# A two-layer encoder: rotated copies, last-head loads, token chunks and strips issued at other places

## The chip, the cores and the metric

The kernel runs on one core of one Trainium2 chip. The metric is the device time of one execution in microseconds (us); the median of several runs is compared. The core has a matrix engine (TensorE, PE in the profile), a vector engine (DVE), a scalar or activation engine (ACT), a general engine (POOL) and a queue engine (SP) that issues nearly all the DMAs here. Each engine works through its own instructions strictly in the order in which they were put there. An instruction that waits therefore holds up everything behind it on that engine.

## The reference

Two layers over 1024 tokens of width 1024: differential attention with eight heads, then latent attention with eight heads. Each ends in an output projection, a gate and a residual add; a final RMSNorm closes the trunk.

```python
for i in range(DEPTH):
    shift, scale, gate = _modulation(c, ada_w[i], ada_b[i])
    h = _rmsnorm(x, norm_g[i]) * (1.0 + scale) + shift
    y = _diff_attention(...) if i == 0 else _mla(...)
    x = x + gate * y
return _rmsnorm(x, final_norm_g)

def _diff_attention(h, ...):
    q, k, v, z = jnp.split(h @ w_in, 4, axis=-1)   # q and k: two parts of 64 per head, rotated (rope)
    sc = einsum(q, k) * scale
    p = softmax(sc)
    p = p[:, :, 0] - lam * p[:, :, 1]
    o = rmsnorm(p @ v, subln_g) * (1.0 - lambda_init) * silu(z)
    return o @ w_out
```

## The kernel before, in words

**Arithmetic.** A float32 product is made of three matmuls on parts: each operand is split into a high part (a cast on ACT) and a low part (a subtraction, mostly on POOL), and `mm3` (L182 to L184) adds high by high, low by high and high by low. A triple of 128x512 matmuls is the unit in which PE's work is counted below.

**First layer.** The heads, counted from 0, run one after the other. While PE computes scores (L851), transposes of probabilities (L383) and products with the values (`pv`) of head h, a stream of projection triples (`acc`) for head h+1 is mixed in. Each weight strip is fetched by SP (L206), cast on ACT (`wh`, L227) and subtracted on POOL (`wl`, L228). For one row tile of 128 queries, two halves of the softmax follow each other: scores `s` on PE, the maximum on DVE (`nm`, L400), the exponential on ACT (L402), and then DVE joins the two (`e`, L859).

**Rotation.** When half of a head's k or q projection is done, `rope` starts: ACT copies the accumulator out (`rp_raw`), SP issues four DMAs that exchange rows (`rp_sw`, L323), POOL multiplies (L324, L329) and, from head 1 on, adds (L331). Then `stack_q` or `stack_k` makes the operands of the scores: two ACT copies (`qa`, L352 and L353), two POOL subtractions (`qb`, L354 and L355) and four DMAs on SP (L357 and L358, for qa and qb). The scores of a head wait for these DMAs.

**Order.** The steps of a rotation are entries of one list, `side`; each step of the projection stream (one triple) takes one entry off it. An entry `None` passes one step by. From head 1 on, a half puts ten entries on the list, for eight steps of its stream. `hooks` is a second list that is run at later points of the attention loop. Marked instructions keep the program's order on their engine (`in_turn`, `behind`).

**First output projection.** The first layer's `o @ w_out` is computed with seven half-size products instead of eight (class `Seven`, object `sv0`). Operands are fetched (`fetch_a`, `fetch_w`) and split (`split_a`, `split_w`: ACT cast L1173, POOL subtraction L1174; `oah`/`oal` from the attention output, `woh`/`wol` from the weights). `extra0(i)` issues this during the last head of the first layer, step i of eleven; `PRE0[i]` says how many triples of product 0 PE does in that step. When the products are done, `add0` adds them on DVE to the residual (`x`, L1390), `group0` normalises four token tiles (DVE L457 and ACT L455) and puts eight chunks on `side`. A chunk is four transposes on PE (`trh`, L468), an ACT pass (`h1_h`, L473) and a DVE pass with a subtraction (L477, L478). `G_WAIT` empty entries stand ahead of them. Two banks serve the transposes. During product 6 the list is stepped every second triple. The second layer's strips (`w_s1`) are fetched and split here too.

**Elsewhere.** `store_v` casts a tile of values, subtracts and stores it. `load_wk(h)` loads and splits weights for the second layer's keys and values. `qp_done` is the rotation of the second layer's q. At the end `add_to` adds up the last row tiles and `rsqrt8k` computes the root on DVE in seven small instructions; `rsqrt` does it with one power on POOL.

## Time and profile before

| | |
|---|---|
| median of 3 runs | 1430.78 us (1428.41 to 1431.87) |
| profiled execution | 1428.76 us; its span 1427.0 us |
| PE busy | 1382.6 us, 97% of the span, 7350 matmuls |
| DVE / ACT / POOL busy | 937.9 / 737.0 / 751.1 us |
| mean granted TensorE clock | 0.988 |
| bytes moved | 231.55 MB, mean 162 GB/s |

The profiled execution lasted 1.76 us longer than the span that its trace shows. In a timeline row stand the start, the duration, the engine, the line, the operation with output and inputs, and in brackets how long the engine was idle before and what ended that. In a row of the waits stand the engine and operation that waited, what it waited for, and then the total in us, the number of times and the longest. In a row of windows stand the stretch, its length, the busy time of each engine with its number of instructions, the granted clock as a share of full speed, the DMA share and GB/s.

### The profile page before, as it was taken

The numbers are of one execution on the slowest core, as the hardware profiler recorded it, in microseconds if no ns is written. First come the engines' busy times: TensorE is split into PE (matmuls) and PEld (weight loads), VectorE is DVE, ScalarE is ACT, GpSimd is POOL, SyncE is SP. The second block draws the span as 40 slices with busy tenths as digits, with TensorE's granted clock in tenths as the row PEclk, the third lists the DMA queues.
The fourth block names the chain that finished last, engine by engine and source line by source line (L and its number), as shares of the span: only waits on it lengthen the run. The fifth ranks groups of instructions, "written<-read, shape, count | busy, mean of one in ns | idle before, by whom it ended". The sixth has DMA issues, their size and how long they took to land. (4 is left out here: it accounts for less than half of the span.)

```text
span 1427.0 us, 20754 instructions
## 1 busy us (share of the span) xinstructions
PE 1382.6 (97%) x7350; PEld 1154.4 (81%) x7350; DVE 937.9 (66%) x1345; ACT 737.0 (52%) x1331; POOL 751.1 (53%) x589
## 2 busy tenths in 40 slices
PE   8999999999999999999898999999999999999997
PEld 6777788888888787887786888787888888888886
DVE  8665777777666665667496886545665655555685
ACT  5523455656565555566546443335454454545554
POOL 5415274758686767674694233632131165653783
PEclk8999999999999999999999999999999999999999
DMA  9776634343444343525564136498444355566463
GB/s 339 252 241 193 201 104 129 91 132 104 151 125 138 119 136 108 161 62 185 160 231 157 43 87 217 127 302 240 156 124 120 103 165 185 182 211 204 144 243 119
DMA packets 149067, 231.55 MB, mean 162 GB/s; under 512 B 20577, under 2 KB 57569, under 8 KB 148962
## 3 DMA queue, kind: packets, MB, share of 16 engines
q1 hardware_dynamic: 148962, 230.21, 51.2%
q8 instruction: 58, 0.95, 0.3%
q14 instruction: 47, 0.39, 0.1%
HBM read 144.74 MB, written 61.81 MB: 145 GB/s over the span
## 5 line engine op out<-in xcount | busy, mean ns | idle before, releaser
L385 ACT CAST pth<-tr 128x512 fp32r<-128x512 f32 x256 | 150.2, 587 | 298.2 <-PE tr L383 296.3
L400 DVE TENSOR_REDUCE nm<-s 128x1 f32<-128x1024 f32 x192 | 233.9, 1219 | 98.5 <-PE s L851 86.7
L386 DVE TENSOR_TENSOR ptl<-tr,pth 128x512 fp32r<-128x512 f32 x256 | 176.3, 688 | 146.9 <-ACT pth L385 144.8
L228 POOL TENSOR_TENSOR wl<-wraw,wh 128x512 fp32r<-128x512 f32 (+2 forms) x79 | 103.0, 1305 | 200.6 <-ACT wh L227 176.9
L402 ACT ACTIVATE e<-s,nm 128x1024 f32<-128x1024 f32 x128 | 143.5, 1121 | 35.0 <-DVE nm L400 31.6
L383 PE MATMUL tr<-ident,e 128*128 128x128 f32 x1024 | 156.5, 275 | 3.3 <-DVE ptl L386 3.3
L383 PEld LDWEIGHTS tr<-ident,e 128*128 128x128 f32 x1024 | 122.3, 141 | 45.8 <-DVE ptl L386 21.2
L182 PE MATMUL acc<-h0h,wh 128*128 128x512 f32 x360 | 151.4, 420 | 0.4 <-DVE v_hl L363 0.3
L182 PE MATMUL pv<-pth,vt 128*128 128x256 f32 x512 | 147.4, 288 | 0.0
L183 PE MATMUL pv<-ptl,vt 128*128 128x256 f32 x512 | 145.6, 284 | 0.0
L184 PE MATMUL pv<-pth,vt 128*128 128x256 f32 x512 | 144.6, 282 | 0.0
L184 PE MATMUL acc<-h0h,wl 128*128 128x512 f32 x360 | 143.1, 398 | 0.8 <-POOL wl L228 0.8
L183 PE MATMUL acc<-h0l,wh 128*128 128x512 f32 x360 | 142.1, 395 | 0.0
L324 POOL TENSOR_TENSOR rp_r<-rp_raw,cosT 128x512 f32<-128x512 f32 x38 | 49.7, 1309 | 103.4 <-ACT rp_raw L321 43.8
L183 PEld LDWEIGHTS pv<-ptl,vt 128*128 128x128 f32 x512 | 97.7, 191 | 3.0
L182 PEld LDWEIGHTS pv<-pth,vt 128*128 128x128 f32 x512 | 97.6, 191 | 2.9
L184 PEld LDWEIGHTS pv<-pth,vt 128*128 128x128 f32 x512 | 97.6, 191 | 0.1
L851 PE MATMUL s<-ks,qa 128*128 128x512 f32 x256 | 84.2, 410 | 11.6 <-DMA qa<-qa 6.9
L1174 POOL TENSOR_TENSOR wol<-wol,woh 128x512 fp32r<-128x512 f32 x56 | 82.2, 1490 | 21.2 <-ACT woh L1173 21.1
L859 DVE SCALAR_TENSOR_TENSOR e<-s,z,e 128x1024 f32<-128x1024 f32 x64 | 82.2, 1284 | 2.2
L851 PE MATMUL s<-ks,qb 128*128 128x512 f32 x256 | 81.2, 398 | 0.5 <-DMA qb<-qb 0.5
L184 PEld LDWEIGHTS acc<-h0h,wl 128*128 128x128 f32 x360 | 67.7, 188 | 16.7 <-POOL wl L228 1.3
(410 smaller groups left out, 3477.4 us busy)
## 6 DMA issues: line engine op xcount, KB each, us to landing
ada<-in_ada_ss SPq DMA_DIRECT2D x32, 512.0 KB, 5.6
wraw<-in_w_s SPq DMA_DIRECT2D x64, 256.0 KB, 2.9
vS<-v_hl SPq DMA_DIRECT2D x32, 512.0 KB, 5.9
vt<-vS SPq DMA_DIRECT2D x32, 512.0 KB, 4.9
wol<-tS SPq DMA_DIRECT2D x56, 256.0 KB, 5.1
tS<-ob SPq DMA_DIRECT2D x48, 256.0 KB, 2.0
rp_sw<-rp_raw SPq DMA_DIRECT2D x168, 64.0 KB, 2.0
bc_s<-bc_d SPq DMA_DIRECT2D x34, 256.0 KB, 3.9
```

The costliest lines, as they stand in the source:

```text
L182: PE.matmul(psum, ah, bh, start=first, stop=False, skip_group_check=skip)
L183: PE.matmul(psum, ah, bl, start=False, stop=False, skip_group_check=skip)
L184: mm3.last = PE.matmul(psum, al, bh, start=False, stop=last, skip_group_check=skip).ins
L228: sub = (V if pair_of else G).tensor_sub(l_[:, :n], raw[:, :n], f32v(h_[:, :n]))
L383: transpose_p.last = PE.transpose(tr[:, j, :], p[:, kt * P : (kt + 1) * P], ident).ins
L385: mk["S"] = S.copy(pth[kh][:, :, dst], tr).ins
L386: mk["V"] = V.tensor_sub(ptl[kh][:, :, dst], tr, f32v(pth[kh][:, :, dst])).ins
L400: mk["V"] = V.reduce_max(nm, s_ps, axis=AX.X, negate=True).ins
L402: mk["S"] = S.activation(e, s_ps, AF.Exp, bias=nm, scale=1.0, accum_out=zs).ins
L851: PE.matmul(s_ps[:, kc * HF : (kc + 1) * HF], src[:, c, ql], KS[h][kc][:, c, :], start=fst, stop=not fst)
L859: combined.append(V.scalar_tensor_tensor(out=e0, in0=e1, scalar=z1[:, 0:1], in1=e0, op0=ALU.mult, op1=ALU.add).ins)
L1174: sub = eng.tensor_sub(lo, raw, f32v(hi))
```

## The change

The edits, with their places:

- `k_done`, `q_done`: the two entries `sum_` are gone, so the copies come two steps sooner.
- `extra0`, `PRE0`, `head_out`: the first fetches of product 0 stand one step earlier, splits are issued at other steps, and the last head's first root (`rest`) is issued behind the splits of its step instead of in `hooks`.
- `G_WAIT` from 3 to 5; the first two strips of `w_s1` are fetched together, two tiles in the buffers `wraw`, two in those of `gz`.
- `store_v` of the first v tiles uses six buffers of another tag; halves of q are projected one v tile later; two tags of the pool `a0b` are allocated ahead.
- `load_wk(1)` moves behind a later part of the same stage; the rotation's add of `qp_done` is on POOL for head 0, half 1.
- The last row tile's root is a power on POOL.

```diff
-PRE0 = (0, 0, 0, 0, 1, 2, 2, 2, 2, 2, 3)
+PRE0 = (0, 0, 0, 0, 1, 2, 2, 2, 3, 2, 2)
-G_WAIT = 3
+G_WAIT = 5
-        store_v(0, p1b, vacc[tt], 4 + tt, 0)
+        store_v(0, p1, vacc[tt], 4 + tt, 0, "xt", 6)
...
-                stack_q(qa, qb, r.pop() if r else fin())
+                stack_q(qa, qb, fin())
                 QS.setdefault(h, [None, None])[half] = qa, qb
-            r = []
-            sum_ = [lambda: r.append(fin()), None] if h else []
-            side.add(*[None] * ROT, rot, *[None] * (DEF - 1 - ROT), *sum_, g)
+            side.add(*[None] * ROT, rot, *[None] * (DEF - 1 - ROT), g)
...
-        for t in pend[4 + 2 * tt : 6 + 2 * tt]:
+        for t in pend[2 + 2 * tt : 4 + 2 * tt] if tt else ():
...
-        if dst is None and h < NH - 1:
-            hooks.append(rest)
+        if dst is None:
+            (hooks if h < NH - 1 else rests).append(rest)
...
+        if i == 1:
+            sv0.fetch_w(0, 0)
...
-            for h in range(2):
-                fw(0, h)
-                fa(0, h)
+            fa(0, 0, 1)
+            fw(0, 1)
+            sv.split_w(0, 0)
         if i == 3:
+            sv.split_a(0, 0, G)
...
-        for n, h in ((), (), (), ((0, 0),), ((0, 1), (0, 2)), ((0, 3), (1, 0)), ((1, 1),), ((1, 2),), (), (), ())[i]:
+        for n, h in ((), (), (), (), ((0, 1), (0, 2)), ((0, 3),), ((1, 0), (1, 1)), ((1, 2),), (), (), ())[i]:
             both(n, h)
+        while rests:
+            rests.pop(0)()
...
             if i == 1 and n == 5:
+                raws = [[], []]
                 with tc.issue_after(w6):
-                    raws = fetch_strip([A["w_s1"][0, f] for f in range(2)], [4, 4])
-            if i == 0 and n == 6:
-                w4.append(split_strip(raws))
-            if i == 1 and n == 6:
-                raws = fetch_strip([A["w_s1"][1, f] for f in range(2)], [4, 4])
-            if i == 3 and n == 6:
-                w4.append(split_strip(raws, h1p))
+                    for k, (tag, nb) in enumerate((("wraw", 2), ("gz", 3))):
+                        for f in range(2):
+                            raw = wst.tile([P, HF], F32, name="wraw", tag=tag, bufs=nb)
+                            SP.dma_start(raw, A["w_s1"][k, f])
+                            raws[k].append((raw, 4))
+            if i > 1 and n == 6:
+                w4.append(split_strip(raws.pop(0), h1p if i == 3 else None))
...
+            load_wk(1)
     z_pair(1)
-    load_wk(1)
...
-            rot, fin = rope(wp, acc, half, SC1)
+            rot, fin = rope(wp, acc, half, SC1, G, V if h or not half else G)
...
-        if early:
+        if tt == NT - 1:
+            y = rsqrt(w, 1)
+            G.tensor_scalar(y, y, -8192.0, None, op0=ALU.mult)
+            scale(tt, y[:, 0:1])
+        elif early:
             scale(tt, rsqrt8k(w)[:, 0:1])
```

The lines of the kernel after are shifted by up to eight against the kernel before.

SP ahead of head 4, in the kernel before: `qa_4113` and `qb_4114` are the first half's operands, `rp_sw_4101` the second half's exchanged rows.

```order
L206 DMA wraw_4074<-in_w_s0 128x512
L323 DMA rp_sw_4101<-rp_raw_4100 32x512 x4
L357 DMA qa_4113<-qa_4113 64x512
L358 DMA qa_4113<-qa_4113 64x512
L357 DMA qb_4114<-qb_4114 64x512
L358 DMA qb_4114<-qb_4114 64x512
```

The same stretch of SP now, with `qa_4078` and `qb_4079` for the first half:

```order
L206 DMA wraw_4076<-in_w_s0 128x512
L357 DMA qa_4078<-qa_4078 64x512
L358 DMA qa_4078<-qa_4078 64x512
L357 DMA qb_4079<-qb_4079 64x512
L358 DMA qb_4079<-qb_4079 64x512
L323 DMA rp_sw_4113<-rp_raw_4112 32x512 x4
```

The first half's four DMAs now stand ahead of the second half's four exchanges.

ACT at the same place before, where `e_4050` and `s_4076` are the two exponentials of one row tile:

```order
L402 ACTIVATE e_4050,zz_3860<-s_4043,nm_4048 128x1024
L227 CAST wh_4068<-wraw_3835 128x512
L385 CAST pth_3980<-tr_4090 128x4x128
L402 ACTIVATE s_4076,z1_4042<-s_4076,nm_4081 128x1024
L321 ACTIVATE rp_raw_4100<-acc_3991 128x512
L352 CAST qa_4113<-rp_r_3968 64x512
L353 CAST qa_4113<-rp_r_3968 64x512
```

And now:

```order
L402 ACTIVATE e_4052,zz_3862<-s_4045,nm_4050 128x1024
L227 CAST wh_4070<-wraw_3837 128x512
L352 CAST qa_4078<-rp_r_3975 64x512
L353 CAST qa_4078<-rp_r_3975 64x512
L385 CAST pth_3982<-tr_4102 128x4x128
L402 ACTIVATE s_4088,z1_4044<-s_4088,nm_4093 128x1024
L321 ACTIVATE rp_raw_4112<-acc_3993 128x512
```

The two copies, which read POOL's sum, moved ahead of the cast of transposed probabilities and of the second exponential.

POOL in the last head before, where `rq_y` is the root and `wol_6758` the low part that a triple of product 0 reads:

```order
L919 TENSOR_TENSOR o_6890<-o_6890,gz_6486 128x512
L169 TENSOR_TENSOR rq_y_6905<-sl_w_6899,mhalf_109 128x4
L934 TENSOR_TENSOR rq_y_6905<-rq_y_6905,sl_f_6900 128x4
L1174 TENSOR_TENSOR oal_6913<-k11_6666,oah_6912 128x512
L1174 TENSOR_TENSOR wol_6758<-wol_6758,woh_6757 128x512
```

And now, with `wol_6764` for the same part:

```order
L917 TENSOR_TENSOR o_6892<-o_6892,gz_6498 128x512
L1172 TENSOR_TENSOR oal_6898<-k11_6671,oah_6897 128x512
L1172 TENSOR_TENSOR wol_6764<-wol_6764,woh_6763 128x512
L169 TENSOR_TENSOR rq_y_6913<-sl_w_6907,mhalf_109 128x4
L932 TENSOR_TENSOR rq_y_6913<-rq_y_6913,sl_f_6908 128x4
```

The two subtractions passed the root.

ACT around the first chunks in the first output projection before, where `wh_7815` to `wh_7923` belong to the first two strips and `wh_8213` to the third:

```order
L227 CAST wh_7815<-wraw_7713 128x512
L227 CAST wh_7819<-wraw_7715 128x512
L473 ACTIVATE h1_h_7729<-trh_7731,modb1_105,moda1_104 128x512
L1394 ACTIVATE tjunk_7742,ss1_7182<-x0_6_7177 128x512
L473 ACTIVATE h1_h_7759<-trh_7761,modb1_105,moda1_104 128x512
L227 CAST wh_7919<-wraw_7861 128x512
L1394 ACTIVATE tjunk_7775,ss1_7182<-x0_7_7178 128x512
L227 CAST wh_7923<-wraw_7863 128x512
L473 ACTIVATE h1_h_7783<-trh_7785,modb1_105,moda1_104 128x512
L227 CAST wh_8213<-wraw_8209 128x512
```

And now, where `wraw_8211` is the third strip's raw tile:

```order
L227 CAST wh_7875<-wraw_7715 128x512
L227 CAST wh_7921<-wraw_7719 128x512
L227 CAST wh_7879<-wraw_7717 128x512
L1397 ACTIVATE tjunk_7737,ss1_7184<-x0_6_7179 128x512
L227 CAST wh_7925<-wraw_7721 128x512
L227 CAST wh_8215<-wraw_8211 128x512
L1397 ACTIVATE tjunk_7759,ss1_7184<-x0_7_7180 128x512
L473 ACTIVATE h1_h_7767<-trh_7769,modb1_105,moda1_104 128x512
```

All of the casts, the third strip's first one too, now stand ahead of the first chunk's pass.

## The prediction

> **What bounds the kernel now.** I read the top of the page first, then the waits of PE, then the granted clock in short windows behind PE's longest pauses, and last the timelines of the engines at each pause.

> ```profile
> span 1427.0 us, 20754 instructions
> PE 1382.6 (97%) x7350; PEld 1154.4 (81%) x7350; DVE 937.9 (66%) x1345; ACT 737.0 (52%) x1331; POOL 751.1 (53%) x589
> ```

> PE is busy for 1382.6 of 1427.0 us, and no edit adds or removes a matmul. The change can act only on the 44.4 us in which PE stands, and on stretches in which it runs slowly. The waits of PE (in all, times, longest) say what ends the pauses:

> ```profile
> PE s L851 <- DMA qa<-qa: 6.9, 4, 2.9
> PE tr L383 <- DVE ptl L386: 3.3, 6, 0.9
> PE s L851 <- DVE e L859: 3.2, 3, 2.4
> PE oy L183 <- POOL wol L1174: 2.5, 1, 2.5
> PE vps L182 <- DVE v_hl L363: 1.7, 1, 1.7
> PE vps L182 <- DVE gz L786: 1.4, 1, 1.4
> PE zacc L184 <- POOL wl L228: 0.9, 1, 0.9
> PE s L851 <- DMA qb<-qb: 0.5, 1, 0.5
> ```

> The first and last rows are the starts of heads 4 to 7, 7.4 us together. The third and fourth are mostly the last head. Some pauses cost more than themselves, as the windows after two of them show (the third figure from the right is the granted clock), and the length of the matmuls themselves:

> ```profile
> 490.00:492.50 2.50, 2.44 (x13) 2.03 (x14) 0.43 (x1) 0.11 (x1) 2.32 (x2) 1.00 0.06 18
> 562.00:564.00 2.00, 2.00 (x7) 1.43 (x6) 0.00 (x0) 0.00 (x0) 1.92 (x2) 0.50 0.37 139
> 564.00:566.00 2.00, 2.00 (x11) 1.67 (x11) 0.95 (x1) 0.59 (x1) 0.55 (x1) 0.86 0.00 0
> ```

> ```profile
> 490.06 0.70 PE L851 MATMUL s<-ks,qa 128*128 128x512 f32 x2 [2.24 <-DMA qa<-qa]
> 561.51 1.19 PE L851 MATMUL s<-ks,qa 128*128 128x512 f32 x2 [2.93 <-DMA qa<-qa]
> 663.55 1.22 PE L851 MATMUL s<-ks,qa 128*128 128x512 f32 x2 [2.40 <-DVE e L859]
> 683.55 0.50 PE L183 MATMUL oy<-wol,oah 128*128 128x512 f32 x1 [2.52 <-POOL wol L1174]
> 684.62 1.05 PE L851 MATMUL s<-ks,qa 128*128 128x512 f32 x2
> ```

> A pause of 2.24 us left the clock at 1.00, and a pair of score matmuls took 0.70 us. After 2.93 us the clock was 0.50, and the pair took 1.19; it took 1.22 after 2.40 us, and 1.05 just behind the pause of 2.52. So those three pauses were followed by half clock. From the two windows after 562 such a stretch loses 2 x 0.50 + 2 x 0.14 = 1.3 us, and I use 1.3 us for each of the three. [...]

> **The change, part by part: the rotation's copies.** In the four waits of 6.9 us and the one of 0.5 us, the four DMAs stood on SP behind the second half's exchanges, and POOL's subtractions behind its next multiplication:

> ```profile
> 556.30 1.29 POOL L355 TENSOR_TENSOR qb<-rp_r,qa 64x512 fp32r<-64x512 f32 x1
> 557.85 0.59 SPq L358 DMA_DIRECT2D qa<-qa  x1
> ```

> Now both subtractions pass that multiplication, which is of their own size (1.29), so they end at 556.3 instead of 557.6, and qa is issued as soon as ACT has copied. PE stood ready at 558.58 (561.51 less 2.93). The last of qa was issued at 557.85 and let PE start at 561.51, 3.7 us later; by that, a qb issued at 556.3 arrives near 560.0, and PE asks for it 0.5 us after qa, at 559.1. I leave 0.3 of the wait (0 to 0.9, since at 419 one wait for qb was as short as 0.5). The gain is 7.4 - 0.3 = 7.1 us, and the cold stretch after 561 goes, 1.3 more: 8.4.

> The copies also pass instructions on ACT, and there they can wait for POOL's sum L331. Head 4 is the place:

> ```profile
> 404.08 0.62 ACT L227 CAST wh<-wraw 128x512 fp32r<-128x512 f32 x1
> 406.44 1.10 ACT L402 ACTIVATE s<-s,nm 128x1024 f32<-128x1024 f32 x1
> 407.47 1.28 POOL L331 TENSOR_TENSOR rp_r<-rp_r,rp_sw 128x512 f32<-128x512 f32 x1
> 411.02 0.63 PE L851 MATMUL s<-ks,qa 128*128 128x512 f32 x2
> ```

> POOL's order ahead of L331 is unchanged in length, so ACT, free at 404.70, stands until 408.75. Two copies of 0.62, a cast of 0.58 and the exponential (1.1, read-out 0.2) follow: it ends near 411.8 instead of 407.7. Queued behind it are DVE's join L859 (some 1.7 with its small steps) and the scores of 411.02, which need its bank: 413.5. That is a new pause of 2.5 us (0 if POOL comes sooner, 4.2 and a cold stretch of 1.3 at worst). At head 6 the same move costs nothing:

> ```profile
> 549.94 1.30 POOL L331 TENSOR_TENSOR rp_r<-rp_r,rp_sw 128x512 f32<-128x512 f32 x1
> 553.45 1.12 ACT L402 ACTIVATE e<-s,nm 128x1024 f32<-128x1024 f32 x1
> ```

> The sum is there at 551.24, two copies end at 552.5, ahead of the exponential at 553.45. Part one: 8.4 - 2.5 = **+5.9** saved (2.3 to 8.7).

> **The last head.** Two stalls, each with a cold stretch behind it:

> ```profile
> 659.94 0.62 ACT L1173 CAST woh<-wol 128x512 fp32r<-128x512 f32 x1 [0.80 <-DMA wol<-tS]
> 660.47 1.08 ACT L402 ACTIVATE s<-s,nm 128x1024 f32<-128x1024 f32 x1
> 679.77 1.01 POOL L169 TENSOR_TENSOR rq_y<-sl_w,mhalf 128x4 f32<-128x4 f32 x1 [2.04 <-DVE sl_w L932]
> 682.82 1.28 DVE L859 SCALAR_TENSOR_TENSOR e<-s,z,e 128x1024 f32<-128x1024 f32 x1
> ```

> The cast waited 0.80 us for its DMA in front of an exponential that could have begun at 659.14. With the fetch a step earlier it stands ahead of the exponential before, so DVE's join and the scores of 663.55 come 1.33 us sooner. The 1.07 us pause that stays is below 2.24, so I drop its cold stretch: 1.3 + 1.3. At 683.55 PE waited for `wol`, behind a root that waited for DVE. The subtractions now pass the root; but the scores behind that triple need the bank that DVE frees at 682.82 + 1.28 = 684.10, against 684.62. Of 2.52 us only 0.5 becomes time, and a pause near 2.0 stays, at which I drop the second cold stretch too. Part two: 1.3 + 1.3 + 0.5 + 1.3 = **+4.4** (1.8 if the clock still falls at both, 7 if the chain also moves up).

> **The first output projection.**

> ```profile
> 759.76 3.43 DVE L457 TENSOR_SCALAR x<-x,rq_y 128x1024 f32<-128x1024 f32 x2 [1.20 <-POOL rq_y L169]
> 763.12 1.87 DVE L1390 TENSOR_TENSOR x<-x,oy 128x512 f32<-128x512 f32 x3
> 763.59 0.78 PE L182 MATMUL oy<-woh,oah 128*128 128x512 f32 x1
> 771.31 0.47 PE L182 MATMUL oy<-woh,oah 128*128 128x512 f32 x1
> 771.78 0.62 ACT L227 CAST wh<-wraw 128x512 fp32r<-128x512 f32 x1 [2.33 <-DMA wraw<-in_w_s]
> 776.54 0.66 PE L468 MATMUL trh<-ident,x 128*128 128x128 f32 x4 [1.77 <-DVE h L477]
> 786.01 0.40 PE L182 MATMUL acc<-h_h,wh 128*128 128x512 f32 x1
> ```

> Today two pauses of PE on L457 stand ahead of 763.59. They go as waits, but product 6 cannot begin before DVE's first add has freed its bank, a third of the way through the row at 763.12: near 763.7, as now. One pause of some 4 us takes the place of two.

> Two triples then precede each group of transposes. Now PE got from 763.59 to 771.31 with five triples and two groups, most of it at a slow clock; six and two bring it to the third group at 772.0. That group needs a bank that ACT's first pass and then DVE's must free, and ACT's pass now stands behind the third strip's cast. Now that cast waited until 771.78 for a buffer and its DMA, and POOL still frees the buffer behind the same subtractions. With a pass on each engine behind it, some 0.8 each, the bank is free near 774.8: a pause of 2.8 us, cold after it, 1.3. From the row at 776.54 to the strip at 786.01 PE needed 9.5 us for four groups and ten triples; six groups and ten triples (a group is 0.35 more) reach the strip at 785.0. So 1.0 saved and 1.3 lost: **-0.3** (-3.5 if the cold stretch is as long as the one after 763.59, +2 if the DMA lands sooner).

> **The rest.** `load_wk(1)` and the add on POOL take the work away that stood ahead of the waits of 0.9 and 1.7 us: 2.6 at most, **+2.0** since DVE gets two casts elsewhere (0 to 2.6). The stores of the first v tiles and the later halves of q bear on the 1.4 us wait on gz: **+0.5** (-1 to +2). For the last root:

> ```profile
> L169 POOL TENSOR_TENSOR rq_y<-xss,mhalf 128x1 f32<-128x1 f32 x1 | 0.6, 553 | 0.0
> 1419.38 0.16 DVE L2173 SCALAR_TENSOR_TENSOR tw<-tss,tw 128x1 f32<-128x1 f32 x1
> 1421.90 0.75 DVE L2187 SCALAR_TENSOR_TENSOR x<-x,rq_y,fg 128x512 f32<-128x512 f32 x1
> ```

> POOL, idle there, takes 0.55 and a short multiply from 1419.54, ready near 1420.4. Both rows' products (0.75 each) then end about 0.5 sooner than 1422.65: **+0.5** (-0.5 to 0.8). Against all this I set new small waits, since every head's order changed; the present ones on ptl are 3.3 us in six: **-1.5** (-4 to 0).

> **The sum.** 5.9 + 4.4 - 0.3 + 2.0 + 0.5 + 0.5 - 1.5 = 11.5 us saved. Against the profiled execution's 1428.76 us (its span and 1.76 us around it) that is 1417.3; it lay 2.0 below the median of the three runs, so **1419.3 us** as a median. The parts' bounds, taken as independent of each other, make about 1414.6 to 1426.2 of this case.

> **Rivals.** *The softmax chain takes over (0.12).* At heads 5 to 7 the scores, no longer late for qa, wait for DVE's join instead, as at 684. For it: the 3.2 us on L859. Against: while streams run, those waits are only in the last head. Part one's 8.4 is lost: 11.5 - 8.4 = 3.1, 1427.7, no measurable change.

> *The third strip's cast blocks more (0.13).* If its DMA lands later than 771.78, both banks stay taken: 2 us more pause and a cold stretch twice as long make about -5 instead of -0.3, so 6.8 saved, 1424.0.

> *ACT stands at many heads (0.11, slower).* The pause of head 4, 2.5 with a cold stretch of 1.3, recurs at the moved copies of k and q, fourteen places. It decides where ACT arrives more than the 1.6 us of slack (411.02 less 409.4, the join's end) ahead of POOL's sum. Five further places and head 4's own cold stretch cost 5 x 3.8 + 1.3 = 20.3, leaving 8.8 us more than before: 1439.6; with three it is no change. For it: POOL's sum comes 4 us late at head 4. Against: head 6 above.

> *The copies are not really sooner (0.06).* POOL or SP still sets qb's landing and only half of the 8.4 is had: 7.3 saved, 1423.5.

> **How the numbers follow.** The forecast has 0.58. A measurement here tells a change from none at about 0.3%, 4.3 us. Faster: 0.58 + 0.13 + 0.06 = 0.77; the same: 0.12; slower: 0.11. The range runs from 1410, below the case's own 1414.6 by what a warm first projection and no head-4 pause would add together, to 1430, which takes in every case but the slower one.

> **What would show it.** Right: no wait on DMA qa above 1 us, clock 1.00 in the windows after heads 6 and 7 begin and after 663 and 684, no wait of PE on `wol`. A pause of about 2.5 us near 411 on L859, while head 3 runs, with ACT idle before L352 on POOL L331. One pause of 4 us at 760 and one near 772 on the transposes. Wrong: waits on L859 at the starts of heads 5 to 7, ACT idle on L331 at several heads, or half clock where I dropped it.

## The result, and the profile after

The kernel after took 1431.31 us (median of 14 runs, 1428.85 to 1436.29), the kernel before 1431.09 us (14 runs on the same chips). The ratio is 1.0001, with a 95% interval of 0.9988 to 1.0015: no change that can be measured. The forecast was 1419.3 us, with a range of 1410 to 1430.

The top of the page and PE's waits of the kernel after (in all, times, longest):

```profile
span 1426.9 us, 20750 instructions
PE 1380.7 (97%) x7350; PEld 1150.1 (81%) x7350; DVE 937.0 (66%) x1337; ACT 737.9 (52%) x1331; POOL 753.9 (53%) x592
```

```profile
PE tr L383 <- DVE ptl L386: 9.7, 11, 2.2
PE trh L468 <- DVE h L477: 4.5, 1, 4.5
PE s L847 <- DVE e L855: 4.1, 7, 1.0
PE ssq L924 <- ACT rp_raw L321: 2.5, 1, 2.5
...
PE vps L182 <- DVE gz L782: 1.3, 1, 1.3
```

The waits on DMA qa (6.9 us) are gone, as forecast, and of the wait on `wol` (2.5 us) 0.6 us is left, at two places. In their place PE waits on `ptl`, the low part of the transposed probabilities: 9.7 us instead of 3.3. The cause stands in the waits of ACT, of before first and then of after:

```profile
ACT qa L352 <- POOL rp_r L331: 2.2, 2, 1.6
ACT ks L344 <- POOL rp_r L331: 1.0, 2, 0.7
```

```profile
ACT qa L352 <- POOL rp_r L331: 23.3, 11, 4.8
ACT ks L344 <- POOL rp_r L331: 8.2, 5, 3.4
```

ACT now stands 31.5 us at 16 places ahead of a moved copy, because POOL's sum is not there yet. One place, in head 0 while head 1's q is rotated, shows how that reaches PE. The timeline of the kernel before, and then of the kernel after:

```profile
206.60 1.12 ACT L402 ACTIVATE e<-s,nm 128x1024 f32<-128x1024 f32 x1 [0.61 <-DVE nm L400]
206.71 1.28 POOL L331 TENSOR_TENSOR rp_r<-rp_r,rp_sw 128x512 f32<-128x512 f32 x1
...
210.74 0.62 ACT L352 CAST qa<-rp_r 64x512 fp32r<-64x512 f32 x1
```

```profile
206.51 0.59 ACT L385 CAST pth<-tr 128x512 fp32r<-128x512 f32 x1 [2.67 <-PE tr L383]
...
210.57 1.29 POOL L331 TENSOR_TENSOR rp_r<-rp_r,rp_sw 128x512 f32<-128x512 f32 x1
...
211.90 0.62 ACT L352 CAST qa<-rp_r 64x512 fp32r<-64x512 f32 x1 [4.80 <-POOL rp_r L331]
...
212.42 1.11 ACT L402 ACTIVATE e<-s,nm 128x1024 f32<-128x1024 f32 x1
...
214.28 1.09 ACT L402 ACTIVATE s<-s,nm 128x1024 f32<-128x1024 f32 x1
...
216.13 1.28 DVE L855 SCALAR_TENSOR_TENSOR e<-s,z,e 128x1024 f32<-128x1024 f32 x1
...
217.33 0.68 DVE L386 TENSOR_TENSOR ptl<-tr,pth 128x512 fp32r<-128x512 f32 x1
...
218.07 0.66 PE L383 MATMUL tr<-ident,e 128*128 128x128 f32 x4 [2.24 <-DVE ptl L386]
```

Before, both exponentials stood ahead of the copy, and by then the sum was long there. After, ACT waits 4.80 us for it with both exponentials queued behind: their maxima (`nm`, L400 on DVE) ended at 208.64 and 210.37, and they started only at 212.42 and 214.28. DVE's join, `ptl` and PE's transposes follow late, and PE stands 2.24 us.

The sum itself also came later: it began at 206.71 before and at 210.57 after. It needs the exchanged rows, and their DMAs now stand on SP behind the first half's `qb`, which waits for the first half's subtractions. SP's issues, before first and then after:

```profile
199.79 2.42 SPq L323 DMA_DIRECT2D rp_sw<-rp_raw  x4
```

```profile
204.64 0.46 SPq L358 DMA_DIRECT2D qb<-qb  x1
205.20 2.44 SPq L323 DMA_DIRECT2D rp_sw<-rp_raw  x4
```

The exchanges went out 5.4 us later, of which 1.1 us is the later start of the heads. So at this place the move did two things: it put the copy ahead of the exponentials, and it made the sum late that the copy waits for.

What the eight heads cost is read from a landmark: the distance from the first product with the values of head 0 to that of head 7. Before it is 654.69 - 174.33 = 480.36 us, after it is 487.23. The rows of the kernel after:

```profile
175.43 0.28 PE L182 MATMUL pv<-pth,vt 128*128 128x256 f32 x1
...
662.66 0.36 PE L182 MATMUL pv<-pth,vt 128*128 128x256 f32 x1
```

So the heads lost 6.9 us where I forecast a gain of 5.9, and the other parts of the change gave it back.

### The profile page after: what moved, and what is told of

It reads as the page before. It is cut to its first block, busy times and chain, and to the rows that moved or that the text cites. A ratio compares the mean times of both kernels' runs of the same rounds, so it can differ in the third digit from the quotient of the medians.

```text
span 1426.9 us, 20750 instructions
## 1 busy us (share of the span) xinstructions
PE 1380.7 (97%) x7350; PEld 1150.1 (81%) x7350; DVE 937.0 (66%) x1337; ACT 737.9 (52%) x1331; POOL 753.9 (53%) x592
## 4 chain that ended last, share of the span: by engine, by line
PE 70%; DVE 5%; POOL 5%; ACT 3%; DMA 3%; issue 2%; SPq 2%; POOLq 0%; ACTq 0%; DVEq 0%
PE s L1986 10%; PE acc L182 8%; PE acc L184 8%; PE acc L183 8%; PE tr L383 7%; PE s L847 6%; PE pv L182 3%; PE pv L184 3%; PE pv L183 3%; PE zacc L184 1%; PE zacc L183 1%; PE zacc L182 1%; PE oy L184 1%; PE oy L182 1%; PE oy L183 1%
## 5 line engine op out<-in xcount | busy, mean ns | idle before, releaser
L400 DVE TENSOR_REDUCE nm<-s 128x1 f32<-128x1024 f32 x192 | 233.9, 1219 | 77.4 <-PE s L847 68.1
L386 DVE TENSOR_TENSOR ptl<-tr,pth 128x512 fp32r<-128x512 f32 x256 | 176.1, 688 | 148.5 <-ACT pth L385 147.9
L228 POOL TENSOR_TENSOR wl<-wraw,wh 128x512 fp32r<-128x512 f32 (+2 forms) x79 | 102.1, 1295 | 185.0 <-ACT wh L227 180.8
L383 PE MATMUL tr<-ident,e 128*128 128x128 f32 x1024 | 155.8, 274 | 10.0 <-DVE ptl L386 9.7
L383 PEld LDWEIGHTS tr<-ident,e 128*128 128x128 f32 x1024 | 120.4, 140 | 54.3 <-DVE ptl L386 31.5
L402 ACT ACTIVATE e<-s,nm 128x1024 f32<-128x1024 f32 x128 | 143.6, 1121 | 26.5 <-DVE nm L400 26.2
L182 PE MATMUL acc<-h0h,wh 128*128 128x512 f32 x360 | 150.6, 418 | 0.1
L182 PE MATMUL pv<-pth,vt 128*128 128x256 f32 x512 | 147.5, 288 | 0.0
L183 PE MATMUL pv<-ptl,vt 128*128 128x256 f32 x512 | 145.5, 284 | 0.0
L184 PE MATMUL pv<-pth,vt 128*128 128x256 f32 x512 | 144.6, 282 | 0.0
L184 PE MATMUL acc<-h0h,wl 128*128 128x512 f32 x360 | 143.2, 398 | 0.4 <-POOL wl L228 0.4
L183 PE MATMUL acc<-h0l,wh 128*128 128x512 f32 x360 | 142.1, 395 | 0.0
L183 PEld LDWEIGHTS pv<-ptl,vt 128*128 128x128 f32 x512 | 97.6, 191 | 2.9
L182 PEld LDWEIGHTS pv<-pth,vt 128*128 128x128 f32 x512 | 97.4, 190 | 3.1 <-ACT pth L385 0.2
L184 PEld LDWEIGHTS pv<-pth,vt 128*128 128x128 f32 x512 | 97.6, 191 | 0.0
L329 POOL TENSOR_TENSOR rp_sw<-rp_sw,sinT 128x512 f32<-128x512 f32 x42 | 57.3, 1365 | 73.8 <-DMA rp_sw<-rp_raw 72.8
```

The lines of the kernel that those rows point to most:

```text
L182: PE.matmul(psum, ah, bh, start=first, stop=False, skip_group_check=skip)
L183: PE.matmul(psum, ah, bl, start=False, stop=False, skip_group_check=skip)
L184: mm3.last = PE.matmul(psum, al, bh, start=False, stop=last, skip_group_check=skip).ins
L228: sub = (V if pair_of else G).tensor_sub(l_[:, :n], raw[:, :n], f32v(h_[:, :n]))
L383: transpose_p.last = PE.transpose(tr[:, j, :], p[:, kt * P : (kt + 1) * P], ident).ins
L386: mk["V"] = V.tensor_sub(ptl[kh][:, :, dst], tr, f32v(pth[kh][:, :, dst])).ins
```

## The experiments

All twelve ran in three groups of four, each kernel beside the kernel before (medians 1432.34, 1433.38 and 1432.55 us in the three). The interval of each ratio reaches 0.0012 to 0.0025 to each side, some 2 to 3.5 us. Versions of different groups are compared by the ratios as well as by the medians.

**Undo the moved copies.** Both lists, from head 1 on:

```diff
-side.add(*[None] * ROT, rot, *[None] * (DEF - 1 - ROT), g)
+side.add(*[None] * ROT, rot, *[None] * (DEF - 1 - ROT), *[None] * (2 if h else 0), g)
```

> The kernel after, with two empty entries put back ahead of the copies of k and q from head 1 on, so that they stand where they stood in the kernel before; all other parts of the change stay. Theory (the moved copies make ACT stand for POOL's sum, 31.5 us of ACT idle at 17 places in the trace after, and the softmax behind them comes late): by the landmarks the heads lost 5.6 to 6.9 us, so undoing it gives about 1424.5 us; ACT waits on the sum fall back to about 2 us in all and PE's waits on ptl from 9.7 to about 3. Rival one (the copies are worth the 5.9 us that I forecast and another part, the first v tiles or the buffers allocated ahead, costs what was lost): slower than after, about 1437. Rival two (the copies matter to nothing, gains and losses at the heads cancel): 1431.

Measured: 1423.68 us, ratio 0.9947 (0.9928 to 0.9965). The landmark distance is back at 480.80 us. PE's waits in its trace:

```profile
PE s L847 <- DMA qa<-qa: 6.5, 4, 2.1
...
PE tr L383 <- DVE ptl L386: 3.2, 6, 0.9
```

ACT's waits on the sum fall from 31.5 us at 16 places (the expectation says 17) to 4.0 us at four, the DMA waits are back, and the kernel is 7.6 us faster than after (7.7 by the ratios, 1.0001 against 0.9947). Both rivals fall: the copies do matter, and no other part holds the loss.

**Only the moved copies.** The two entries `sum_` are taken out of both lists of the kernel before; nothing else is changed.

> The kernel before, with the copies of k and q two steps sooner from head 1 on, and no other part of the change. Theory (ACT stands): 5.5 to 7 us slower than before, about 1437; ACT waits on the sum near 30 us, PE waits on DMA qa gone, waits on ptl near 10. Rival one (the copies gain as forecast): 1425. Rival two: 1431, the waits on qa being replaced by as much waiting on ptl and e.

Measured: 1444.45 us, ratio 1.0074 (1.0049 to 1.0098), a landmark distance of 491.69 us. The sign is the theory's; the size, 12.1 us by the medians, is more than its 5.5 to 7. ACT's and PE's waits are those of after:

```profile
ACT qa L352 <- POOL rp_r L331: 24.2, 11, 4.8
...
PE tr L383 <- DVE ptl L386: 9.4, 9, 2.2
```

The trace holds three more half-clock stretches of 3.41 us within the heads than the trace of after (four, from 217.95, 415.92, 419.34 and 583.18, against the one from 417.95), from nearly the same pauses (the last section shows one). By the estimate there they are 5.1 us, and the 7.0 us that remain are the upper end of what the theory gave.

**One entry instead of two.** `*[None] * (1 if h else 0)` in both lists of the kernel after.

> The kernel after, with one of the two empty entries put back: the copies come one step later than after and one step sooner than before. Theory (ACT stands): the idle time of ACT on the sum has a mean of 1.9 us at a place; one step of the stream is 2 us or more, so most of it goes, and SP still issues qa and qb sooner than before: 1422 to 1426, at or a little below the version with both entries. Rival one (copies gain the more the sooner): half of its gain is lost against after, 1434. Rival two: 1431.

Measured: 1426.68 us, ratio 0.9963 (0.9950 to 0.9975). ACT still waits much, and one DMA wait of 2.7 us is left:

```profile
ACT qa L352 <- POOL rp_r L331: 18.6, 8, 6.2
ACT ks L344 <- POOL rp_r L331: 7.1, 5, 2.5
...
PE s L847 <- DMA qa<-qa: 2.7, 1, 2.7
```

It is faster than after but not better than two entries. I had thought that one step would clear most of the waits; it cleared 5.8 of 31.5 us. That step of my reasoning was wrong, though the direction is the theory's. The longest wait even grew:

```profile
424.19 0.62 ACT L352 CAST qa<-rp_r 64x512 fp32r<-64x512 f32 x1 [6.17 <-POOL rp_r L331]
```

Here too the exchanges of the second half stand behind the first half's `qb`: ACT had copied the rows out at 412.32, and SP issued their exchanges at 417.32. An entry put ahead of the copies does not bring the sum back to its old time. No run takes the two effects apart.

**Only q's first half moved.** k and q's second half get the two entries back: `(2 if h and half else 0)` for q, `(2 if h else 0)` for k.

> The kernel after, with the two empty entries put back for both halves of k and for the second half of q: only the first half of q, whose DMAs stood behind the second half's exchanges, is still copied two steps sooner. Theory (ACT stands): the 8.2 us of ACT idle on k and about half of the 23.3 on q go, the waits on DMA qa stay away: between the versions with no and with all copies moved, 1424 to 1428. Rival one: 1433. Rival two: 1431.

Measured: 1422.34 us, ratio 0.9927 (0.9915 to 0.9939), lower than I expected and in one range with the version that has every copy undone. ACT still waits 9.5 us at seven places for the sum, and one DMA wait of 1.5 us is left.

**Take the wait away, not the place.** In `rot` of the kernels after and before:

```diff
-in_turn(G.tensor_add(r, r, sw))
+in_turn(G.tensor_mul(sw, sw, cosT[:, cs]))
```

> The kernel after, with POOL's sum of the rotation from head 1 on (r = r + sw) replaced by a multiplication of the same shape on another tile (sw = sw * cos), so POOL keeps its work and its order while ACT's copies read the first product and need not wait for the sum. What is left out: the second half of the rotation of q and k in the first layer, from head 1 on. Theory (what costs is ACT standing for the sum): the 31.5 us of ACT idle go, the copies keep their early place, the waits on DMA qa stay away too; the loss of the copies (7.6 us between the versions with both entries and with none) goes and the gain appears: 1417 to 1421. Rival (the place itself costs: two copies of 0.62 us ahead of an exponential and of the transposed probabilities, at every head): no better than 1428 to 1431.

> The same replacement in the kernel before, as the measure for the one above; the same half of the rotation is left out. There ACT waited only 2.2 us for the sum, and SP's order is unchanged. Both theories: 1428 to 1432, within 0.3% of before. If it is faster by more than 4 us, taking away the sum itself is worth time and the kernel above must be read against this one.

Measured: 1418.93 us in the kernel after (ratio 0.9900, 0.9885 to 0.9915) and 1432.63 us in the kernel before (0.9997, 0.9983 to 1.0012). Both kernels leave the rotation's sum out from head 1 on. POOL does as much as ever and the copies keep their early place, yet the kernel after now takes 12.4 us less (14.5 by the ratios). The landmark distance is 478.40 us. The two waits on the sum are gone from ACT's list. Two waits on POOL's first product have come in their place, and PE has one large wait left in the heads, on DMA qa, where I had expected none; what held that DMA is not shown. ACT's row, and then PE's:

```profile
ACT qa L352 <- POOL rp_r L324: 5.5, 2, 4.5
```

```profile
PE s L847 <- DMA qa<-qa: 4.5, 1, 4.5
...
PE tr L383 <- DVE ptl L386: 2.8, 5, 0.8
```

This is the pair that shows the cause: what costs is ACT's wait for the sum in front of the softmax, not the two copies in that place. It also shows that the early copies are worth something when they don't wait: 1423.68 - 1418.93 = 4.8 us (6.7 by the ratios).

**Moved from head 5 on only.** As q's first half, with `(2 if h and (half or h < 5) else 0)`.

> As the version with only the first half of q moved, but moved from head 5 on only; heads 1 to 4 keep the old place. In that version's trace, ACT's stand ahead of head 4 left PE a pause of 1.96 us at 411.8 with slow matmuls behind it, while the old place cost head 4 two DMA waits of 1.14 and 0.53 us. Theory (each stand is paid where the softmax has no slack): 0 to 2 us better than that version, 1420 to 1422.5. Rival (heads 1 to 4 gain from the earlier copies too): 1423 to 1424.

Measured: 1420.65 us, ratio 0.9908 (0.9893 to 0.9923); a landmark distance of 476.54 us. It is faster than both kernels of this case: it lies 12.7 us below the kernel before in its own group, and after is as fast as before. Against the version with q's first half moved in every head, the intervals overlap, and heads 1 to 4 are not separated. The text on record speaks of slow matmuls behind the pause at 411.8; the windows there show a clock of 1.00, so that part of it was a misreading.

**The first v tiles undone**, in the version with q's first half moved: the stores, the order of `pend` and the two tags as before.

> The version with only the first half of q moved, with the edits at the first v tiles undone as well (buffers of the stores, halves of q projected one tile later, the two tags allocated ahead). I had given these edits a gain of 0.5 us. By the landmark of the first product with the values, the four traces with the edits stand 0.6 to 1.9 us later than before, from starts that differ by 1.5 us themselves. If they cost 1.4 us: 1421. If they gain 0.5 as forecast: 1422.8.

Measured: 1424.35 us, ratio 0.9936 (0.9924 to 0.9949), 2.0 us slower than the version with the edits, with intervals that overlap. The edits gain, if anything, more than the 0.5 that I gave them; the loss of 1.4 that I read from the landmarks was not there. The run with the edits undone is 2.28 us late at the same landmark, so that stretch differs by such sizes from run to run.

**The other parts undone, one by one**, in the version moved from head 5 on: the last head's order; three entries and the strips' old steps (`G_WAIT` and the fetches); the place of `load_wk(1)` and the add on DVE.

> The version with the first half of q moved from head 5 on, with the last head's fetches, splits, root and triples in their old order. My term was 4.4 us; the landmarks of the four versions that have the new order show 3.5 to 4.3 us between the last product with the values of the head before and the second product of the projection. If that holds: 1424 to 1425. If the gain is given back before the first output projection: 1421.

> The version with the first half of q moved from head 5 on, with three empty entries ahead of the chunks and the first two strips fetched and split at their old steps. My term was a loss of 0.3 us; the landmarks on both sides of this stretch show from 1.5 us gained to 1.2 us lost in four versions. So 1419.5 to 1421.5 if the term was right; 1424 if the part saves as much as the two removed waits on L457 (2.9 us).

> The version with the first half of q moved from head 5 on, with the loads and splits of the second pair of key weights at their old place and the rotation's add of the first head's second half of q on DVE again. My term was 2.0 us; the landmarks from 862 to 1040 us show 1.1 to 2.0 us. So 1422 to 1423 if it holds, 1420.7 if not.

Measured: 1426.09 us (0.9955, 0.9941 to 0.9970), 1423.38 us (0.9936, 0.9920 to 0.9953) and 1422.24 us (0.9930, 0.9915 to 0.9944). So the parts are worth 5.4, 2.7 and 1.6 us by the medians and 6.7, 4.0 and 3.1 us by the ratios. The first is clear; the other two are of the size of their intervals. With the last head undone, its old waits are back:

```profile
PE s L847 <- DVE e L855: 3.8, 4, 2.7
PE oy L183 <- POOL wol L1172: 3.1, 3, 2.5
```

**Chunks one entry sooner**: `G_WAIT` 4 in the version moved from head 5 on.

> The version with the first half of q moved from head 5 on, with four empty entries ahead of the chunks of tokens in the first output projection instead of five. ACT's pass over the first chunk then stands ahead of the cast that waits for the third strip's DMA (3.14 us of ACT idle at 774.2 in the trace after), not behind it. Theory (the pause of 4.5 us on the transposes is the pass standing behind that cast): the pause falls by 2 us or more and its slow matmuls with it, 1417 to 1419. Rival (the strip's own lateness or DVE, with its adds in front of its pass, would hold PE anyway): 1420 to 1422.

Measured: 1419.89 us, ratio 0.9914 (0.9896 to 0.9932). The pause on the transposes fell as the theory said, from 4.37 us to this:

```profile
763.74 1.08 PE L468 MATMUL trh<-ident,x 128*128 128x128 f32 x4 [2.03 <-DVE h L477]
```

The time didn't follow: it is 0.8 us lower by the medians and no lower by the ratios (0.9914 against 0.9908), within both intervals. The mechanism of the pause is shown, a gain in time is not.

## Why the prediction was wrong, step by step

**The rotation's copies, forecast +5.9, measured -7.6** (after against the version with the copies undone). This is the step that failed. Its first half was right: the DMA waits of 7.4 us went, all but 0.3. The wrong step is "At head 6 the same move costs nothing", from which I took head 4 to be the only place. I had costed the stand of ACT at two places and let the one without it stand for the rest. Even at head 6 it did not hold: the same copy now waits for a sum that ends at 561.23, and PE stood 0.67 us on `ptl` at 564.41.

```profile
561.27 0.62 ACT L352 CAST qa<-rp_r 64x512 fp32r<-64x512 f32 x1 [1.97 <-POOL rp_r L331]
```

In the whole kernel there were 16 such places, 31.5 us of ACT in all, and PE got four pauses above 1 us in these heads that neither the kernel before nor the undone version has: 2.24, 1.12, 2.50 and 1.60 us at 218.07, 222.87, 416.04 and 481.30. The copies of k and of q's second half, which moved just as far, had no DMA wait to win and only the wait on POOL to lose; I had not costed them in the sum at all. I had also left out that the swap on SP, which I counted as the gain, makes the second half's exchanges later. The second halves of q are 15.2 of the 31.5 us. The pause ahead of head 4 itself came as forecast in size, 2.50 us against 2.5:

```profile
416.04 1.05 PE L924 MATMUL ssq<-ones,osq 128*128 128x1 f32 x8 [2.50 <-ACT rp_raw L321]
```

It came through another instruction, the accumulator's copy `rp_raw`, queued on ACT behind the same stand, so that the match of the size is partly luck. The window behind it, from 417.95 to 421.36, ran at a clock of 0.50; the sum had priced that stretch only at worst.

**The rival "ACT stands at many heads", given 0.11,** named the mechanism and its fourteen places. It fails on its price: five further places at 3.8 us and a cold stretch, 20.3 us, where the copies' term fell by 5.9 + 7.6 = 13.5 us. The rest of the change was worth about what I gave it (the last paragraph of this section), and so the copies' loss and its gain met at no change. Its condition, ACT arriving more than 1.6 us ahead of the sum, told more than my argument against it.

**The last head, +4.4.** Undoing it costs 5.4 us. In the kernel after, head 7's first product with the values came 7.97 us late (662.66 against 654.69); the first triple of the projection's second product came 3.65 late:

```profile
708.29 0.40 PE L182 MATMUL oy<-woh,oah 128*128 128x512 f32 x1
```

The same triple stood at 704.64 before, so 4.3 us were won. Both stretches of half clock went: between 421.37 and 776.35 the clock is 1.00 throughout. This step was right.

**The first output projection, -0.3.** Undoing it costs 2.7 us (not separated from zero). Two readings in it were wrong and cancel in part. The single pause of 4 us near 760 did not come; PE waited only 0.45 us there. The pause on the transposes was larger than 2.8, since the third strip's cast waited for its DMA until 774.24, the second rival's mechanism:

```profile
766.15 0.47 PE L182 MATMUL oy<-woh,oah 128*128 128x512 f32 x1 [0.45 <-DVE x L1393]
...
777.04 1.12 PE L468 MATMUL trh<-ident,x 128*128 128x128 f32 x4 [4.50 <-DVE h L477]
```

```profile
774.24 0.62 ACT L227 CAST wh<-wraw 128x512 fp32r<-128x512 f32 x1 [3.14 <-DMA wraw<-in_w_s]
```

**The rest.** `load_wk(1)` and the add, +2.0: 1.6 us by the medians, right within the interval. The first v tiles, +0.5: 2.0 us, the upper bound. The last root, +0.5: from its last product to the end the kernel after gained 0.2 us, which the timing cannot tell from nothing. New small waits, -1.5: with the copies undone, the waits on `ptl` are 3.2 us against 3.3 before, so this term was nothing, or part of the copies' loss. Without the copies I forecast 7.1 us for the other parts (4.4 - 0.3 + 2.0 + 0.5 + 0.5); together they gave 1432.34 - 1423.68 = 8.7 (7.6 by the ratio). The four parts undone singly sum to 11.7, which is no contradiction at 2 to 3 us of uncertainty each.

## What to carry to other kernels

Before an instruction is moved ahead of others on its engine, find for every copy of the move when its operand is ready and when the engine gets there; one place where it fits says nothing of the others. Look also at what the moved instructions feed: here their DMAs passed the ones that a later operand needs. Where the operand comes from another engine, here POOL's sum of 1.29 us, the wait for it can be charged to what is queued behind: the wait of 4.80 us at 211.90 stood ahead of two exponentials. Move only the instances that have a wait to win: of the choices of copies tried here that compute the reference, the first half of q from head 5 on had the lowest median, though it is not separated from the first half of q in every head.

## What the runs showed of the hardware

All of this is read from the traces of seven kernels of this case: before, after, the copies undone, only the copies moved, only q's first half moved, the sum taken out of after, and the chunks one entry sooner.

```profile
216.56:219.97 3.41, 1.90 (x11) 1.64 (x12) 3.41 (x4) 1.10 (x2) 2.76 (x2) 1.00 0.26 59
219.97:223.38 3.41, 2.29 (x13) 1.63 (x12) 3.41 (x5) 1.13 (x2) 0.02 (x1) 1.00 0.73 232
```

```profile
214.54:217.95 3.41, 1.17 (x7) 0.69 (x6) 2.75 (x5) 2.02 (x5) 1.83 (x3) 1.00 0.50 115
217.95:221.36 3.41, 3.41 (x11) 2.73 (x10) 3.41 (x4) 0.58 (x1) 1.55 (x2) 0.50 0.50 156
```

In the first, PE stood 1.5 us of its window and the next stayed at 1.00; in the second it stood 2.24 us, and the next ran at 0.50 throughout. In the seven traces, from 20 to 1400 us, all 18 windows at full clock with 2.0 us or more of standing were followed by half clock, and none of the 2764 with less than 1.5 us was; of the 14 between 1.5 and 1.8, four were. The first 20 us do not fit: in the kernel after PE stood 0.02 us of the window from 4.94, and half clock followed; that stays open. An edge of the grid cut the 2.24 us pause of before at 490.06 into 1.65 and 0.6, which fits its warm end, and my line between 2.24 and 2.40 us was no line at all. By an estimate from the length and the clock, a cold stretch in which PE is busy throughout costs 3.41 x 0.50 = 1.7 us, not the 1.3 that I used. The runs of one program differ by several such stretches: the mean clock of the six runs of the version with only the copies moved went from 0.982 to 0.991, and one stretch is 1.7 / 1444.5 = 0.0012, so by that estimate they are some seven or eight stretches apart. That a run's phase against the grid does this is my reading; no run shows it. By the same estimate three more stretches are 5.1 of the 12.1 us of that version.
